# First block of x normed in two token halves, the gate's two bank readers put in a fixed order, and the last output weights spread over three rings

## The chip, the cores and the metric

The kernel runs on one core of one Trainium2 chip. The metric is the device time of one execution in microseconds. The names of the engines: PE is TensorE (matrix products; its weight loads are listed apart as PEld), DVE is VectorE, ACT is ScalarE, POOL is GpSimd, and SP is SyncE, which only issues transfers. Each engine works through its own queue in the order in which the program lists the instructions; engines wait for each other through semaphores.

## The reference

The program is one layer of a hybrid decoder trunk: 4096 tokens of width 1024, float32.

```
h = rmsnorm(x, norm_w);  u = h @ w_in
GLA   (4 heads): log_a = log_sigmoid(lr @ gate_up + bias) / 16
                 o = chunked gated linear attention(q, k, v, log_a);  o = rmsnorm(o) * silu(g)
RWKV7 (8 heads): token shift, low-rank decay w and rate a,
                 S_t = S_{t-1}(diag(w) - kk^T (a kk)) + v^T k;  y_t = S_t r_t
                 y = groupnorm(y) + bonus;  y = y * silu(g)
out = rmsnorm(x + concat(GLA, RWKV7) @ w_out, final_norm_w)
```

What matters here is that the input projection needs the normed x of a block, that the norm of a token needs a sum over all 1024 columns of that token alone, and that the gate of the linear attention is a log-sigmoid, which the kernel builds from min(z, 0) and from ln(1 + exp(-|z|)).

## The kernel before, in words

Tokens are processed in 8 blocks of 512 (`TB`). x is held transposed: a block is 8 tiles (`KT`) of 128 columns by 512 tokens. The product with float16 operands is kept accurate by splitting each operand into a high and a low float16 part: a projection of 128 output columns is three passes (high by high, high by low, low by high) over 8 tiles, and each step is two matmuls of 128x64 weights by 512 tokens that share the array (`both`, L894 in the profile; L833 is the helper that records every other instruction).

Weights come raw from memory in 29 pieces of 512 KB in the first block. Each is scaled by a power of two of its absolute maximum (an ACT pass over it, `wo<-x` in the profile since it uses an output buffer as scratch; a small PE transposition `bank<-identb,amW`; a few one-column DVE instructions that end in `scl`), split into high and low (ACT writes the high part `wr` or `wg`, DVE the low part), and stored to memory (`wdr`) for the seven later blocks. The raw tiles use the room of the second block's x (they appear as `x<-in_wt_dram`). RWKV weights go through the ring `wr` of two pairs, GLA weights through the ring `wg` of two pairs, output weights through the ring `wo` of two.

The first block's x is loaded in 8 tiles (named `mgg` and `mgr`, whose room it borrows), squared by ACT, summed over columns by PE, put through a reciprocal square root of seven DVE instructions (`newton`), spread over 128 partitions by PE, multiplied in by DVE, cast to the high part by ACT; the low part is a subtraction by DVE for even tiles and POOL for odd ones. Later blocks do the same with other loads, out of the way.

Per block there are then: the RWKV units (4 per block, `rwkv_ab`), whose chunked recurrence `rwkv_c` is a chain of small products with copies between them (`us`, `uv` by ACT, `sv` by DVE, all on bank `ch`); the GLA pairs (2 per block, `gla_proj` and `gla_pair`); and the output projection (`out_block`). The last block has its own output stage `out_last`, which multiplies the first six merged tiles while the last two units' chains are still running and adds the other two tiles at the end.

In `gla_pair` the gate is read twice from one bank of PSUM: DVE makes `gbc` = min(z + b, 0), and ACT makes `gep` = |z + b|, then exp and ln. The framework does not let two engines read one bank at the same time; the one whose instruction comes second in the program waits for the other.

The order of the program is not that of the code. Every instruction is first recorded as a step with what it depends on; a table (`ORDER`) holds a rank for each step, and the program is written out by taking, of the steps whose predecessors are out, the one of lowest rank. A second table (`STARTS`, counted by `COUNTS`) fixes how the streams (x, weights, RWKV, chain, GLA, output) interleave while steps are recorded. Both tables are data in the kernel. The first transfers out of the inputs, `lead`, are kept in their order; all other input loads come after them.

Of the kernel before, what the change touches and what calls it, by code (L numbers as in the profile page):

```python
# [27 lines left out]
TB = 512  # L28
C = 64
SPARE = 0.45  # L30
LAND = {"wdr": 1.5, "in": 1.7, "td": 1.3, "nd": 2.4, "kd": 2.2, "gd": 1.9}
ND = 20
NW = {"r": 4, "g": 4, "o": 2}
# [22 lines left out]
    "c-qx{2bd&f)oxXFoSZl3yeykoU<pf(lA}ll!2k#%2&hC81_VU~R1iTF$%;ylAIxC-$s*taE^%R5Hs_h?xplVQW509etE%pq;oj%&^VD`vb%igU_?~lydY+dFk3x9-r>CdK4?mNRVtC}kV<?Ud;XU=?=l_PErSO;;"  # L56
    "exHYHYr^A(@Z8bir~LNw@K_%na$iSyJQIFDKK%Se_&F~8{9E`LgrBE{M=m_>4F9e*?_U$1YcS_lhUc2ix#i)xw(zqa&ysU5h36)l>s}1cO*7~I6`q@sG7fV5IlOKd#!uf7;4?$l4RPEX;F`4<^E}SwF*e7A$L-;7"
    "AH@05;c;*H_g>*=_|bEr>2m@1O1qy8f0Open7)SRZxJ3Z;QPq%Sd6iriu2j<b3}N&5q_6;O$v{HW3F1m<6+!8Cp={Qvv{XG>kd3CgQJKxNqgF8Oal5%k8$Sjy6})S(vG$q7Jfbwe(sFl_YA*(Cp=E1=MKSpb?r#I"
    "zKu4?Sk~hAuJBwp`jNxma{d&Ylk0yI9<ynF<ovYo_ZM+a*3W$yUu|<eeyhPD=f;}$JuMp`{P!7La|Xt6GL20w=2^ba46l{;eG_9m9QVmJjkreo){gJXO3_-mJG^Hf%-1KdR<;U1r-YxY!q1Hu7a8X>%zkg8?^(>9"
    "KY*hpJa)zS$XaMd`}4FGM&MKa{#*t0r;;OxIbV-CZ9xCKK(l;|;|h$89OH3qhxycT56rrj&$)gyZnMLOj>0_Y+LV3ya!+)A60UzV{Cj(>_aBCbT)QuxCu4Pf_?)Z#=<i3v<FDc0<LRAB2ix&3A2eA%ziP%agL&1q"  # L60
    "XK9@m@Lkr+hj8w8+@Gmp>>KG_>%#koW6cf2cnd#}J`BUWx1%3F3y+=fzAVj`>m4_R*PTv0=+`ud9Tl`uX;2r9kF5PC!s7$sxwp{X8t{UoXYG{ou6mlUBg5l|3D3*Y9Lb(PDm-osuNVGSz}(CL?HU0ZeqVRAW_j&@"
    "BPfqyV}<iJqQdKBOm-iHJu1hI{n*z>R?v?_AaBUu6T|U&9W+qJZ7%lVgW)j-<K0Gk;*#*VJp64NSqnJ#Eyy(un7?MC`N|Xb4v&S9O@`yQBf{gl@SLoXKZKuOs)D|?IL?Xe(?R@RK1Z3q?S7A=hk3_udHR&Leh<I%"
    "9t-Gw!n?1J>C?W3*GpSgLC%wPJQ3@>0rJ~5J-un0w&gI$mNP(4WPXK*i(K<;%6M)=G)_LJVBY>f_vyS(BKoesO`^8TnmV1vKxt(_^r{{Fd<m_s5@gP=ho8#Zo9Ny3ShK+(?J1U{<a0-wuef)-8Z(ZqXshzPMPX+e"
    "tK<hsN7nq^8MY&jcedia3n05bjeWNXGU0RKr|1oH9Q=7Yo^ek2`wrkWDg$4cvSwNhy(yZ%WiDR{pRpgElXdXz@bkBzGe_ec>mB+_+A$KJwFx?djN9STf6(`-(4~_2PbEhy`XYMZ67Zd!{D?1?AS=t~AF7~Zg+X4|"
    "gLMcm_#XN(gvRy=$k4ZlJb-==$Gpq>oI^U~5wwQ)509UkapCooiJ4EK8T0Wj;j6crXS5jEDgYhZ2paP!XwW{;Zx;|<S{i<C!1s~Rr-l-3wa0mbBxk1`ho}60{vfZN9j*L`ahEl|m64xL4bR<%^}+OA^`R!{2{Z7$"
    "1%Hd}Vmh9&UHJWz3GK;%J_iYFBkgFQdzlw?l06|w2GGA}IiB54JT7n6OGfqt>CeBZfEJ85^dJkmGzNQ5X!JbLmk#_s6ZWX-ka5)ha3JWp%-uQQ1wQepCE&Alqzlb}t)^0*>7ro=n=!1%-agPg*R{8XnK58lx{2m)"
    "3)ozC7=-;-+mAKnT8Ddv1n^zxrn1&QjL*)<oYC_^KUxbV=qMTVX9TUG_drASnQgRY8@%%U!Y@Ap8Q>P8t)C)Wj{N<3qN}3g9&E-${+2eYU7-{9qyRFg?(I6-KP+=D!@VMBHX2!Z8S(T^^f^zmi_G=sOOc#D0rNW>"
    "*9&bIow~)0xsF*8ynGSHwgG%+HuS)4Np6z1oQm^b!F<01ex)*md_TOWH+{>d%>A?q<TRFn#m;s%uK8AYToL{)a>P(SYWL-(vQ6a#=#Im%Cr=5F=jr#8vDg1rp?nb#f6UM^jqEG!_*-Q8WAJR*yWcmmywy8+KXd<e"
    "4NeO0f8C5l#*F7<uv^MJel<MqFZJ%%HqdQky&e=EXJP*K#n=daJpnT11UzR;+$;LiAx4kkwgg6Il+TBVuk8~aO^$nRr!kPW9D()Ifb%~D?UQF5jWz!hdTthUt;ei87q3zpD0F%ojMc6<C*#qG{Z$KDYd7pCwY{E$"
# [362 lines left out]
def hymba_kernel(ctx, tc, xT, wt, wg, wo, wua, gup, pk, ck, out):  # L432
# [20 lines left out]
    def build(guide):  # L453

        TABLES = ("pkt", "scl", "invs", "hinv", "mu_s", "omu_s", "carry", "wosc", "woinv", "gnh", "lnh")
        FINE = {"Nb": 32, "f": 16}
        HEADS, XS = set(), set()
        now = [0.0]
        streams = []
        ready, used, busy = {}, {}, {}  # L460
# [126 lines left out]

        table = [0]
        steps, wkey, rkey, wlast, readers = [], {}, {}, {}, {}
        last, turn, lead = [None, 0], [0], []  # L590

        class Step:

# [1484 lines left out]
```

## Time and profile before

| | |
|---|---|
| time, median of 3 runs | 2169.9 us (2168.2 to 2171.18) |
| the profiled execution's own time | 2173.05 us |
| its span, first to last instruction | 2171.3 us |
| mean granted clock of TensorE | 0.991 |
| PE busy | 2107.4 us, 97% of the span |
| DVE, ACT, POOL busy | 1615.8, 1277.8, 892.8 us |
| moved by DMA | 322.27 MB, mean 148 GB/s |

How to read what follows: a row of the timeline has the start in us, how long it lasted, engine, source line, operation, what it writes and reads, shapes, count, and in brackets how long the engine had been idle before it and what ended that. `x12` is twelve like instructions run together. A row of the groups has busy us and the mean ns of one after the bar, then the idle time before them and who ended it. Matmuls are pipelined, so a busy PE is not yet PE at its peak.

### The profile page before, as it was taken

The page shows a single profiled execution, that of the slowest core. Times are in us where ns is not written, and L with a number is a line of the kernel's source. Part 1 is how long each engine was busy: PE and PEld are TensorE (multiplying, and loading weights), DVE is VectorE, ACT ScalarE, POOL GpSimd, SP SyncE. Part 2 cuts the span into 40 slices and gives each one's busy share as a digit, 9 for nine tenths or more (in the row PEclk, how much of TensorE's full clock was granted, in tenths as well). Part 3 has the DMA queues.
Part 4 walks back from the last instruction along what each step waited for, and adds up shares of the span by engine and source line. Part 5 has one row for each costly group of instructions (what it writes and reads, how often), then busy time and mean ns, then how long its engine had stood idle before and what let it go on. Part 6 is the DMA issues. An engine that isn't in the chain of part 4 may idle for free.

```text
span 2171.3 us, 68508 instructions
## 1 busy us (share of the span) xinstructions
PE 2107.4 (97%) x27608; PEld 1343.2 (62%) x27608; DVE 1615.8 (74%) x3487; ACT 1277.8 (59%) x3328; POOL 892.8 (41%) x2261
## 2 busy tenths in 40 slices
PE   6998999999999999999999999999999999999997
PEld 2655675565655657557675666656666565756664
DVE  8888979579675786757776687748868578685866
ACT  6777686465645556446664466545575555644552
POOL 4462434545414360545415264341544535254500
PEclk9999999999999999999999999999999999999999
DMA  6667655465344653445444464446533556344532
GB/s 196 203 176 234 207 177 176 137 194 158 94 128 128 189 150 96 133 129 187 144 110 129 135 195 131 126 120 184 163 103 103 162 166 178 88 131 129 151 108 88
DMA packets 271394, 322.27 MB, mean 148 GB/s; under 512 B 129588, under 2 KB 130788, under 8 KB 271076
## 3 DMA queue, kind: packets, MB, share of 16 engines
q1 hardware_dynamic: 271076, 317.89, 49.4%
q8 instruction: 216, 3.54, 0.7%
q14 instruction: 102, 0.84, 0.1%
HBM read 272.74 MB, written 45.05 MB: 146 GB/s over the span
## 4 chain that ended last, share of the span: by engine, by line
PE 80%; DVE 10%; ACT 4%; DMA 3%; issue 2%; POOL 1%; SPq 1%; DVEq 0%; ACTq 0%; POOLq 0%
PE bank L894 63%; PE bank L833 10%; PE ch L894 4%; PE y L894 1%; PE y L833 1%; DVE DD L833 1%; SPq L833 1%; DVE mgg L833 1%; ACT gep L833 1%; DVE bk L833 1%; DVE Nb L833 1%; DMA x<-in_wt_dram 1%; DVE gbc L833 1%; DVE x L833 1%; ACT L833 0%
## 5 line engine op out<-in xcount | busy, mean ns | idle before, releaser
L894 PE MATMUL bank<-x,wr 128*64 128x512 f16 x6528 | 817.0, 382 | 8.1 <-DVE DD L833 1.6
L833 POOL TENSOR_TENSOR tm<-Tc,f 128x60 f32<-128x60 f32 (+24 forms) x961 | 347.9, 362 | 534.6 <-DMA f<-nd 457.8
L894 PEld LDWEIGHTS <-wr 128*64 128x64 f16 x6528 | 360.2, 111 | 265.0 <-issue 26.8
L833 POOL TENSOR_TENSOR Tc<-Tc,tm 128x60 f32<-128x60 f32 (+24 forms) x961 | 359.3, 374 | 73.1
L894 PE MATMUL bank<-x,wg 128*64 128x512 f16 x3072 | 386.1, 381 | 2.4 <-ACT wg L833 1.7
L894 PE MATMUL bank<-x,wo 128*64 128x512 f16 x2976 | 356.1, 380 | 0.4 <-ACT x L833 0.4
L833 DVE SCALAR_TENSOR_TENSOR sv<-ch,PC,psd 64x64 f32<-64x64 f32 x434 | 122.6, 282 | 219.0 <-PE ch L894 185.8
L833 POOL TENSOR_TENSOR xacc<-xacc,xr 128x512 f32<-128x512 f32 x98 | 130.8, 1335 | 336.8 <-ACT xr L833 180.5
L894 PEld LDWEIGHTS <-wg 128*64 128x64 f16 x3072 | 167.6, 110 | 129.1 <-issue 7.9
L894 PEld LDWEIGHTS <-wo 128*64 128x64 f16 x2976 | 162.3, 110 | 120.1 <-issue 1.8
L894 PE MATMUL bank<-wg,x 128*64 128x256 f16 x3072 | 200.3, 273 | 0.3 <-ACT ta L833 0.3
L894 PEld LDWEIGHTS <-x 128*64 128x64 f16 x3168 | 170.4, 110 | 20.0 <-issue 3.4
L833 ACT COPY us<-ch 64x64 f32<-64x64 f32 x496 | 102.3, 206 | 122.7 <-PE ch L894 110.7
L833 ACT ACTIVATE psd<-sv,PC 128x128 f32<-128x128 f32 x248 | 98.8, 398 | 103.6 <-DVE sv L833 80.0
L833 ACT COPY uv<-ch 64x64 f32<-64x64 f32 x496 | 102.4, 206 | 86.4 <-PE ch L894 79.8
L833 ACT ACTIVATE sa<-bank,mu_s 128x512 f32<-128x512 f32 x104 | 71.5, 688 | 70.2 <-PE bank L894 64.3
L833 DVE COPY_PREDICATED Nb<-mc,bank 64x512 f32<-64x512 uint8 x128 | 92.9, 728 | 10.1 <-PE bank L833 8.0
L833 DVE COPY_PREDICATED DD<-mc,bank 64x512 f32<-64x512 uint8 x128 | 93.2, 729 | 2.7 <-PE bank L833 0.2
L833 POOL MEMSET Tc<- 32x8 f32 (+1 forms) x160 | 23.6, 147 | 173.1 <-DMA td<-Tc 167.7
L894 PEld LDWEIGHTS ch<-us,Nb 128*64 128x64 f32 x992 | 65.4, 137 | 42.5 <-ACT us L833 11.2
L894 PEld LDWEIGHTS ch<-uv,bk 128*64 128x64 f32 x992 | 66.8, 137 | 39.8 <-ACT uv L833 8.3
L894 PEld LDWEIGHTS ch<-sv,DD 128*64 128x64 f32 x992 | 66.0, 137 | 38.4 <-DVE sv L833 12.9
(354 smaller groups left out, 3584.0 us busy)
## 6 DMA issues: line engine op xcount, KB each, us to landing
wr<-wdr SPq DMA_DIRECT2D x248, 256.0 KB
xr<-in_xT_dram SPq DMA_DIRECT2D x176, 256.0 KB
wg<-wdr SPq DMA_DIRECT2D x176, 256.0 KB
wo<-wdr SPq DMA_DIRECT2D x128, 256.0 KB
f<-nd SPq DMA_DIRECT2D x128, 128.0 KB
x<-in_wt_dram SPq DMA_DIRECT2D x29, 512.0 KB
wdr<-wo SPq DMA_DIRECT2D x17, 512.0 KB
out_dram<-mgg SPq DMA_DIRECT2D x33, 256.0 KB
```

The lines of the kernel that those rows point to most:

```text
L833: put(t0, self.name, d, lag, cols, tiles, tab, outs, ins, lambda: f(*a, **kw))
L894: nc.tensor.matmul(x, lhsT=l, rhs=y, start=start, stop=stop)
```

## The change

Four things change.

- The first block of x is loaded, squared, summed, normed and split in two halves of 256 tokens (`TH`), by a new function `x_first`. The order of the first loads is: 8 halves (with the parameter table after the first), the first raw weight, the other 8 halves. Two Newton passes of 64 rows replace one of 128. The dependency keys of these tiles tell the two halves apart (`toks`, `TOK`). The first two RWKV projections (`NHALF = 2`) run in halves too, with the low weight before the low x.
- In `gla_pair` ACT's read of the bank is recorded ahead of DVE's. A new rule gives every step by DVE or ACT that reads a bank a dependency on the earlier readers of that bank by the other engine.
- In `out_last` the weights of the eight output columns take turns in the rings `wr`, `wg` and `wo` in place of `wo` alone.
- `ORDER`, `STARTS` and `COUNTS` are new, for the whole program. The counts of steps: RWKV stream 9609 to 9657, x stream 561 to 600, initial loads 35 to 44, weights 582 to 581.

```
-                if len(lead) <= KT:
+                if len(lead) < 2 * KT + 2:
...
+            for a in ins:
+                if a.space == PSUM and eng != "T":
+                    r = bankread.setdefault(a.tensor.name, [])
+                    for m in r:
+                        if m.eng != eng:
+                            s.follow(m, 0.1)
+                    r.append(s)
+            for a in outs:
+                if a.space == PSUM and eng == "T":
+                    bankread.pop(a.tensor.name, None)
...
+        for t in range(0, TB, TH):
+            for k in range(KT):
+                D.dma_start(xfirst[k][:, t:t + TH], xT[P * k:P * k + P, t:t + TH])
+                if k == t == 0:
+                    D.dma_start(pkt, pk)
+            if t == 0:
+                D.dma_start(raws[0], wt[W_WA])
...
+        def x_first():
...
+            for i, q in enumerate((lo, hi)):
+                ts = slice(TH * i, TH * i + TH)
                 ps = yield from need("X")
+                for k in range(KT):
+                    S.activation(sq[k][:, ts], xfirst[k][:, ts], AF.Square)
+                    for g in (2 * i, 2 * i + 1):
+                        T.matmul(ps[32 * g:32 * g + 32, 0:P], lhsT=gones, rhs=sq[k][:, P * g:P * g + P], start=k == 0, stop=k == KT - 1)
+                if i == 0:
+                    yield from norm_weight()
+                y = newton(ps[q, 0:P], 1.0 / DM, 1e-6, None, "g", q)
...
+                for k in range(KT):
+                    t = xfirst[k][:, ts]
+                    V.scalar_tensor_tensor(t, t, nwx[:, k:k + 1], rb[:, ts], ALU.mult, ALU.mult)
+                    S.copy(xs[k][:, 0, ts], t)
+                    (G if k % 2 else V).tensor_tensor(xs[k][:, 1, ts], t, xs[k][:, 0, ts], ALU.subtract)
...
+            early_ = st == "r" and made_r[0] < NHALF
+            made_r[0] += st == "r"
+            if early_:
+                for i in range(2):
+                    ts = slice(TH * i, TH * i + TH)
+                    for n, (a, c) in enumerate(((0, 0), (1, 0), (0, 1))):
+                        for k in range(kt):
...
+                            both(ps[:, ts], w[a][:, k, :], xs[k][:, c, ts], i + n + k == 0, i == 1 and n == 2 and k == kt - 1)
+                return ps
...
             bc, ep = tG("gbc"), tG("gep")
+            S.activation(ep, pz, AF.Abs, scale=gus[:, 5:6], bias=gb)
             V.tensor_scalar(bc, pz, gbz[:, j:j + 1], 0.0, ALU.add, ALU.min)
-            S.activation(ep, pz, AF.Abs, scale=gus[:, 5:6], bias=gb)
...
-                w = yield from get_w(NWT + n, "o")
+                w = yield from get_w(NWT + n, "o", ("r", "g", None)[n % 3])
```

More of the change, by code (lines that the diff above doesn't have):

```diff
@@ L28 @@
 TB = 512
+TH = TB // 2
 C = 64
@@ L32 @@
 ND = 20
+NHALF = 2
 NW = {"r": 4, "g": 4, "o": 2}
@@ L473, in dram, with toks @@
             return [(name, 0)]
+        def toks(ap):
+            t = ap.offset % TB // TH
+            return [t] if len(ap.shape) == 2 and ap.shape[1] <= TH and ap.dtype != BF16 else range(2)
         def parts(ap):
@@ L1902, in stream_w @@
             o = w_order()
-            for n in range(4):
+            for n in range(1, 4):
                 load_raw(n, o[n])
```

745 lines of the change are left out of this document (371 added, 374 removed).

## The prediction

> **What bounds the kernel now.** I read the page first, then the stretches of the start and of the clock drops, then TensorE's idle gaps, then the timeline around each gap.
>
> ```profile
> span 2171.3 us, 68508 instructions
> ...
> PE 2107.4 (97%) x27608; PEld 1343.2 (62%) x27608; DVE 1615.8 (74%) x3487; ACT 1277.8 (59%) x3328; POOL 892.8 (41%) x2261
> ```
>
> TensorE is idle for 2171.3 - 2107.4 = 63.9 us, and only those, with the stretches in which it runs slowly, are on offer. The busy time of stretches (PE, PEld, DVE, ACT, POOL, then granted clock, DMA share, GB/s):
>
> ```profile
> 807.50:810.90 3.40, 3.40 (x22) 1.70 (x20) 1.21 (x3) 3.06 (x7) 2.74 (x9) 0.50 0.00 0
> 1589.10:1592.50 3.40, 3.19 (x22) 1.79 (x24) 1.78 (x3) 3.30 (x8) 2.93 (x7) 0.50 0.00 0
> 2108.00:2111.40 3.40, 3.30 (x28) 1.88 (x28) 0.82 (x3) 1.61 (x8) 0.00 (x0) 0.51 0.09 31
> 0.00:20.00 20.00, 9.19 (x94) 4.17 (x95) 13.49 (x44) 11.37 (x19) 8.64 (x31) 1.00 0.92 262
> 20.00:37.40 17.40, 16.06 (x124) 6.27 (x121) 16.32 (x39) 10.17 (x19) 10.28 (x13) 1.00 0.59 185
> 37.40:47.34 9.94, 2.54 (x29) 0.82 (x24) 7.62 (x31) 9.75 (x18) 1.83 (x1) 0.78 0.25 90
> 47.34:53.10 5.76, 5.76 (x28) 2.56 (x30) 5.60 (x18) 5.68 (x9) 1.36 (x2) 0.50 0.60 161
> ```
>
> So there are two places to gain: the first 53 us (10.8 us idle before 20, 1.3 to 37.4, 7.4 to 47.34, then half clock), and short stalls later which each bring 3.4 us of half clock. In the first 37.4 us VectorE is busy 29.8 us: it bounds the start.
>
> **The change part by part.**
>
> *The gate's reads.* VectorE and ScalarE both read the gate's bank, 16 times. Whichever is listed second waits, and all that is queued behind it on its engine waits too; the old list did not hold that wait.
>
> ```profile
> L833 ACT ACTIVATE gep<-bank,pkt,gus 128x512 f32<-128x512 f32 x16 | 12.4, 775 | 18.4 <-DVE gbc L833 15.6 <-PE bank L894 2.7
> ...
> L833 DVE TENSOR_SCALAR gbc<-bank,gbz 128x512 f32<-128x512 f32 x16 | 11.9, 744 | 5.1 <-ACT gep L833 4.4 <-PE bank L894 0.6
> ```
> ```profile
> 805.00 0.75 DVE L833 TENSOR_SCALAR gbc<-bank,gbz 128x512 f32<-128x512 f32 x1
> ...
> 805.78 0.78 ACT L833 ACTIVATE gep<-bank,pkt,gus 128x512 f32<-128x512 f32 x1 [3.88 <-DVE gbc L833]
> ...
> 807.06 0.34 PE L894 MATMUL ch<-us,Nb 128*64 128x64 f32 x4 [2.48 <-ACT us L833]
> ```
> ```profile
> 1584.11 0.78 ACT L833 ACTIVATE gep<-bank,pkt,gus 128x512 f32<-128x512 f32 x1 [2.32 <-DVE gbc L833]
> ...
> 1589.31 0.48 PE L894 MATMUL ch<-us,Nb 128*64 128x64 f32 x4 [2.12 <-ACT Nb L833]
> ```
> ```profile
> PE bank L894 <- ACT gep L833: 1.1, 2, 0.7
> ```
>
> At 805.78 ScalarE had stood 3.88 us; the chain's copy `us` was behind it, and TensorE stood 2.48 us for that copy. At 1584 the same wait pushed the copies of `Nb` back, 2.12 us of TensorE. Each is followed by 3.4 us at 0.50, worth 1.7 us of lost work. Two more gaps are 1.1 us. Upper bound of the gain: 2.48 + 1.7 + 2.12 + 1.7 + 1.1 = 9.1 us. After the change ScalarE reads first, and VectorE is listed behind its end; behind VectorE's read are queued the chain's `sv` updates. The price of that order shows in the 4.4 us of the second row, and I bound the loss by them, +4. That the waits become visible to whoever made the list does not abolish 0.78 us of ScalarE, so not all comes back: I take **-5.5** (-9.1 to +4).
>
> [...]
>
> *The first block in halves.* Before:
>
> ```profile
> 8.03 0.63 ACT L833 ACTIVATE ta<-mgg 128x512 f32<-128x512 f32 x1 [1.05 <-DMA mgg<-in_xT_dram]
> ...
> 10.64 0.63 ACT L833 ACTIVATE uv<-mgr 128x512 f32<-128x512 f32 x1
> ...
> 12.04 0.29 DVE L833 TENSOR_SCALAR nva<-bank 128x128 f32<-128x128 f32 x1 [2.14 <-PE bank L833]
> 12.13 1.06 ACT L833 ACTIVATE wo<-x 128x1024 f32<-128x1024 f32 x1 [0.86 <-DMA x<-in_wt_dram]
> ...
> 19.17 3.90 PE L894 MATMUL bank<-x,wr 128*64 128x512 f16 x12 [1.40 <-ACT x L833]
> ...
> 28.98 1.28 DVE L833 SCALAR_TENSOR_TENSOR wr<-x,scl,wr 128x1024 f16<-128x1024 f32 x1
> ...
> 30.32 3.86 PE L894 MATMUL bank<-x,wr 128*64 128x512 f16 x34 [0.73 <-DVE wr L833]
> ```
>
> The fourth 256 KB tile, 1 MB in all, was there at 8.03. Eight halves are the same 1 MB, so their last square ends at 8.03 + 0.5 = 8.5. From the last square's end at 11.27 to Newton took 0.77 us; so the first Newton starts at 9.3, some 2.8 us ahead of 12.04. The first raw weight passes 1 MB of x in the list; between 4 and 12 us some 0.3 MB moved per us (rows under the rivals), so it is ready about 3 us ahead of 12.13. The first projection's matmuls thus start near 15 in place of 19.17.
>
> What is added, by the nearest rows of 256 columns:
>
> ```profile
> L833 ACT ACTIVATE guw<-f,gus 128x256 f16<-128x256 f32 x1 | 0.5, 494 | 0.0
> L833 DVE SCALAR_TENSOR_TENSOR guw<-f,gus,guw 128x256 f16<-128x256 f32 x1 | 0.5, 479 | 0.0
> ```
> ```profile
> L833 DVE SCALAR_TENSOR_TENSOR mgg<-mgg,nwx,bank 128x512 f32<-128x512 f32 x5 | 3.5, 739 | 0.0
> ...
> L833 ACT CAST x<-mgg 128x512 f16<-128x512 f32 x5 | 3.0, 614 | 0.2
> ```
>
> VectorE: 16 x 0.48 - 8 x 0.74 = 1.8 us for the products, a second Newton of seven instructions, the first of 0.29 (2 us), some 0.5 us for its four residues in halves: +4.3 us. ScalarE: 16 x 0.49 - 8 x 0.63 for the squares and 16 x 0.49 - 8 x 0.61 for the casts, +5.7 us. GpSimd's four residues become eight; it is idle 11 of the first 20 us. ScalarE has 8.6 us idle in the first 20 us and takes its share there. VectorE has 6.5 idle us there, 2.2 of them between 8 and 12 (1.78 busy of 4, rows under the rivals); leaving out the first 2 us, before any load has landed, some 4 stand against 4.3 added, so VectorE breaks even at 28.98, where the low part of a weight is made. So the gain has to come from TensorE: at 30.32 it still had 16 + 48 matmuls of the first two projections, 64 x 3.86 / 34 = 7 us, in front of the transposes that the third weight's scale waits for, and the part of them whose halves are ready before 30 is now done by then.
>
> The two projections in halves take 192 matmuls of 256 columns for 96 of 512:
>
> ```profile
> L894 PE MATMUL bank<-x,wg 128*64 128x512 f16 x3072 | 386.1, 381 | 2.4 <-ACT wg L833 1.7 <-DVE scl L833 0.4 <-ACT gep L833 0.4
> ...
> L894 PE MATMUL bank<-wg,x 128*64 128x256 f16 x3072 | 200.3, 273 | 0.3 <-ACT ta L833 0.3
> ```
>
> Busy time by count, two of 0.065 us stand for one of 0.126: 96 x 0.004, under 0.4 us.
>
> Then the third projection, where the start loses most:
>
> ```profile
> 42.55 0.75 DVE L833 TENSOR_SCALAR gbc<-bank,gbz 128x512 f32<-128x512 f32 x1 [1.85 <-ACT gep L833]
> ...
> 44.79 0.14 DVE L833 TENSOR_SCALAR scl<-pw 128x1 int32<-128x1 int32 x1
> ...
> 46.15 1.13 ACT L833 ACTIVATE wr<-x,scl 128x1024 f16<-128x1024 f32 x1
> ...
> 47.34 6.27 PE L894 MATMUL bank<-x,wr 128*64 128x512 f16 x30 [0.72 <-ACT wr L833]
> ```
>
> The scale at 44.79 stood behind the gate's read on VectorE, 1.85 us. That is the wait the list now knows. I take that, and as much again for the matmuls done early and the shorter half clock (at most (53.1 - 47.34) / 2 = 2.9): **-3.5**. Bounds: everything lost after 37.4, 7.4 + 2.9 = 10.3 less, and +4.3 if all of VectorE's added work is on the path. On SP eight more issues stand ahead of the second raw weight; its matmuls run after 30.32, so I add nothing for them, and +4.3 holds that too.
>
> *The last output weights.* Two buffers before:
>
> ```profile
> 2100.17 1.86 SPq L833 DMA_DIRECT2D wo<-wdr  x2
> ```
> ```profile
> 2104.75 0.41 PE L894 MATMUL bank<-x,wo 128*64 128x512 f16 x2
> ...
> 2109.00 1.49 PE L894 MATMUL bank<-x,wo 128*64 128x512 f16 x6
> ...
> 2149.95 5.82 PE L894 MATMUL bank<-x,x 128*64 128x512 f16 x48 [0.38 <-DVE mgr L833]
> ```
>
> From 2105.16 to 2109.00 no output matmul runs: two weights are used up and the third was issued at 2100.17. With six sets the third to sixth lie ready. But the last unit's chain ends at 2149.95 in a wait for VectorE, so filler moved forward mostly turns into a wait there. Gain between 0 and 3.84 plus 1.7 of half clock, 5.5; loss bounded by 1, a weight's load that now stands ahead of another transfer. I take **-1**, near the row of 2149.95.
>
> *The new list elsewhere.* It replaces every queue's order. The trace has no row for it. Its gaps outside the rows above (63.9 - 10.8 - 1.3 - 7.4 - 2.5 - 2.1 - 1.1, some 39 us, the end included) can grow or shrink; I bound that by a sixth of them either way, -6 to +6, and take 0, having no row that leans.
>
> Sum: -5.5 - 3.5 - 1 + 0 = -10. The profiled execution took 2173.05 us (span 2171.3 and 1.75 around it), 3.15 over the median of 2169.9: 2173.05 - 10 - 3.15 = **2159.9, forecast 2160**.
>
> **The rivals.**
>
> *Halves that come late.* The first half may not land at 8: it is eight transfers of 128 KB.
>
> ```profile
> 4.00:8.00 4.00, 2.21 (x26) 0.77 (x26) 3.86 (x5) 1.60 (x4) 4.00 (x9) 1.00 0.95 296
> 8.00:12.00 4.00, 3.24 (x40) 1.00 (x40) 1.78 (x12) 3.14 (x5) 0.78 (x5) 1.00 1.08 363
> ```
>
> For it: the DMA engines are full there, share 0.95 to 1.08. Against it: with several tiles in flight the rate is 296 to 363 GB/s, and the bytes are the same. If the rate halves, 1 MB lands 3.5 us later, the 2.8 us are gone and VectorE's 4.3 us stay: the start term is 0, the time 2163.5. [...]
>
> *No change.* The stalls return as planned waits and the start is held by VectorE: gate -1.5, start 0, tail 0, 2168.4. For it: VectorE's 29.8 of 37.4 us; ScalarE stays first at the gate and its queue is as long. Against it: 807.06 and 1589.31 are unplanned stalls of one cause.
>
> *Slower.* VectorE's added 4.3 us and half of ScalarE's 5.7 fall on the path to the third weight, since ScalarE is busy 9.75 of 9.94 us before 47.34: the split of 46.15 comes 7 us later, and 3 us more is lost as the half clock lasts that much longer. With 4 back at the gate: +6, 2176. It decides from where the third projection's dense run starts after 51. Against it: ScalarE's 8.6 idle us earlier.
>
> *Much faster.* All stalls of the gate (-9.1), most of the start (-9): -18, 2152.
>
> **How the numbers follow.** Forecast 0.45, late halves 0.18, no change 0.14, slower 0.14, much faster 0.09. Under 0.2%, about 4.3 us, this kernel's measurement cannot tell from no change. Faster by more: 0.45 + 0.18 + 0.09, less 0.03 of the edges, 0.69; within: 0.14 + 0.03 = 0.17; slower: 0.14. The range leaves out the end of the slow case and of the fast: 2149 to 2175.
>
> **What would show it.** Right: the first 256-column matmul before 16 us; the third projection's run before 44; ScalarE's idle before `gep<-bank` without VectorE as releaser, and no 2 us gap before `us`; no hole in the output matmuls. Wrong: VectorE's idle before `gbc<-bank` over 15 us with `sv` late behind it; the third projection after 51; new TensorE gaps over 1 us away from the gate.

## The result, and the profile after

The changed kernel took **2147.26 us** (median of 4 runs, 2145.91 to 2148.72) against 2169.05 (4 runs, 2167.94 to 2171.18) of the kernel before on the same chip: ratio 0.9898, with a 95% interval of 0.9881 to 0.9916. The gain is 21.8 us, twice the forecast 10, and the time is 1.7 us under the low end of the range. The direction was right.

The head of the page of the changed kernel, and its group rows for the gate (L852 now stands for L833, L913 for L894):

```profile
span 2146.8 us, 68755 instructions
...
PE 2095.0 (98%) x27704; PEld 1351.5 (63%) x27704; DVE 1619.2 (75%) x3506; ACT 1286.9 (60%) x3344; POOL 873.3 (41%) x2265
...
L852 ACT ACTIVATE gep<-bank,pkt,gus 128x512 f32<-128x512 f32 x16 | 12.4, 776 | 8.9 <-PE bank L913 8.7
...
L852 DVE TENSOR_SCALAR gbc<-bank,gbz 128x512 f32<-128x512 f32 x16 | 11.9, 745 | 4.4 <-ACT gep L852 4.1
```

TensorE is idle for 2146.8 - 2095.0 = 51.8 us where it was 63.9, and its busy time fell by 12.4 us although it does as much work. The clock is not the reason: the mean granted clock is 0.991 in the profiled execution of each kernel. What shortened the busy time the profile does not tell. ScalarE no longer waits for VectorE at the gate (15.6 us before), and VectorE's wait for ScalarE did not grow (4.4 before, 4.1 of the 4.4 now). What is left of ScalarE's idle time there is a wait for the matmuls themselves.

The start of the changed kernel, TensorE's timeline:

```profile
15.97 0.52 PE L913 MATMUL bank<-x,wr 128*64 128x256 f16 x6
...
44.43 5.37 PE L913 MATMUL bank<-x,wr 128*64 128x512 f16 x48 [0.70 <-ACT wr L852]
...
53.23 5.15 PE L913 MATMUL bank<-x,wg 128*64 128x512 f16 x32 [3.43 <-ACT wg L852]
...
61.94 0.48 PE L852 MATMUL bank<-DD,bk 64*128 64x128 f32 x2 [1.78 <-DVE bk L852]
...
63.62 3.43 PE L852 MATMUL bank<-DD,bk 64*128 64x128 f32 x30 [1.20 <-DVE bk L852]
```

The first projection starts at 15.97 in place of 19.17 and the third at 44.43 in place of 47.34. Behind them stand three waits, 6.4 us together. In the same place, the kernel before has one of 1.52, and its long wait stands ahead of the third projection:

```profile
46.30 0.32 PE L894 MATMUL bank<-identb,amW 128*64 128x128 bf16 x2 [4.14 <-ACT wo L833]
...
63.00 2.56 PE L894 MATMUL bank<-x,wg 128*64 128x512 f16 x22 [1.52 <-ACT wg L833]
```

The trace alone does not say what each of the four parts is worth; the runs below do.

The kernels named here: `gate_alone` is the kernel before with the gate's part only; names with `undone` are the changed kernel less one part. Where two kernels are compared step by step, the start times of like instructions of ScalarE and VectorE were paired and the median difference taken in each stretch; that is called the lead. It compares one execution of each, not medians.

### The profile page after: what moved, and what is told of

Same layout as the page of the kernel before. It is cut to its first block, busy times and chain, and to the rows that moved or that the text cites. A ratio compares the mean times of both kernels' runs of the same rounds, so it can differ in the third digit from the quotient of the medians.

```text
span 2146.8 us, 68755 instructions
## 1 busy us (share of the span) xinstructions
PE 2095.0 (98%) x27704; PEld 1351.5 (63%) x27704; DVE 1619.2 (75%) x3506; ACT 1286.9 (60%) x3344; POOL 873.3 (41%) x2265
## 4 chain that ended last, share of the span: by engine, by line
PE 85%; DVE 7%; DMA 3%; ACT 2%; issue 1%; SPq 1%; DVEq 0%; ACTq 0%
PE bank L913 68%; PE bank L852 10%; PE ch L913 4%; PE y L852 2%; PE y L913 1%; SPq L852 1%; DVE DD L852 1%; DVE nva L852 1%; DMA wg<-wdr 1%; DVE nta L852 0%; DVE Nb L852 0%; DVE mgg L852 0%; DVE bk L852 0%; DVE x L852 0%; DVE wo L852 0%
## 5 line engine op out<-in xcount | busy, mean ns | idle before, releaser
L913 PE MATMUL bank<-x,wr 128*64 128x512 f16 (+1 forms) x6732 | 831.3, 378 | 3.7 <-DVE DD L852 1.7
L852 POOL TENSOR_TENSOR tm<-Tc,f 128x60 f32<-128x60 f32 (+24 forms) x961 | 347.6, 362 | 622.3 <-DMA f<-nd 465.1
L913 PEld LDWEIGHTS <-wr 128*64 128x64 f16 x6732 | 370.8, 111 | 251.7 <-issue 15.8
L913 PE MATMUL bank<-x,wg 128*64 128x512 f16 x3180 | 397.7, 382 | 4.6 <-ACT wg L852 4.1
L852 POOL TENSOR_TENSOR Tc<-Tc,tm 128x60 f32<-128x60 f32 (+24 forms) x961 | 343.0, 357 | 72.9
L913 PE MATMUL bank<-x,wo 128*64 128x512 f16 x2760 | 328.3, 380 | 0.0
L852 DVE SCALAR_TENSOR_TENSOR sv<-ch,PC,psd 64x64 f32<-64x64 f32 x434 | 122.7, 283 | 222.2 <-PE ch L913 179.7
L913 PEld LDWEIGHTS <-wg 128*64 128x64 f16 x3180 | 176.1, 111 | 133.0 <-issue 6.2
L852 POOL TENSOR_TENSOR xacc<-xacc,xr 128x512 f32<-128x512 f32 x98 | 128.0, 1306 | 299.9 <-ACT xr L852 174.7
L913 PEld LDWEIGHTS <-wo 128*64 128x64 f16 x2760 | 150.1, 110 | 115.5 <-issue 1.9
L913 PE MATMUL bank<-wg,x 128*64 128x256 f16 x3072 | 198.1, 273 | 0.3 <-DMA wg<-wdr 0.3
L913 PEld LDWEIGHTS <-x 128*64 128x64 f16 x3168 | 169.3, 110 | 18.6 <-issue 4.7
L852 ACT COPY us<-ch 64x64 f32<-64x64 f32 x496 | 101.9, 205 | 106.3 <-PE ch L913 95.2
L852 ACT ACTIVATE psd<-sv,PC 128x128 f32<-128x128 f32 x248 | 98.9, 399 | 99.9 <-DVE sv L852 86.1
L852 ACT COPY uv<-ch 64x64 f32<-64x64 f32 x496 | 102.0, 206 | 86.5 <-PE ch L913 78.8
L852 ACT ACTIVATE sa<-bank,mu_s 128x512 f32<-128x512 f32 x104 | 71.4, 686 | 65.2 <-PE bank L913 63.4
L852 DVE COPY_PREDICATED Nb<-mc,bank 64x512 f32<-64x512 uint8 x128 | 93.1, 728 | 7.3 <-PE bank L852 5.2
L852 DVE COPY_PREDICATED DD<-mc,bank 64x512 f32<-64x512 uint8 x128 | 93.4, 730 | 5.4 <-PE bank L852 3.1
L913 PEld LDWEIGHTS ch<-sv,DD 128*64 128x64 f32 x992 | 66.3, 137 | 39.9 <-DVE sv L852 9.4
L913 PEld LDWEIGHTS ch<-uv,bk 128*64 128x64 f32 x992 | 66.7, 137 | 35.8 <-ACT uv L852 3.8
L913 PEld LDWEIGHTS ch<-us,Nb 128*64 128x64 f32 x992 | 66.4, 137 | 35.2 <-ACT us L852 4.0
L913 PE MATMUL ch<-sv,DD 128*64 128x64 f32 x992 | 72.1, 224 | 3.0 <-DVE sv L852 2.2
```

Of the source, the lines that this page charges most:

```text
L852: put(t0, self.name, d, lag, cols, tiles, tab, outs, ins, lambda: f(*a, **kw))
L913: nc.tensor.matmul(x, lhsT=l, rhs=y, start=start, stop=stop)
```

## The experiments

### The gate alone, and the gate put back

`gate_alone` is the kernel before with the two reads swapped and the rule added, on the old list. There VectorE's read stood first at 8 of the 16 gates; at these the two trade places:

```
+            S.activation(ep, pz, AF.Abs, scale=gus[:, 5:6], bias=gb)
             V.tensor_scalar(bc, pz, gbz[:, j:j + 1], 0.0, ALU.add, ALU.min)
-            S.activation(ep, pz, AF.Abs, scale=gus[:, 5:6], bias=gb)
```

> The kernel before, with one part of the change: ScalarE's read of the gate's bank is recorded ahead of VectorE's and the rule for such reads is in; the list is the old one, so at the 8 of 16 gates where the old list had VectorE first, VectorE's read now stands directly behind ScalarE's. Theory G (the gate's order is what paid): the two long stalls, 2.48 and 2.12 us, and their half clocks go, 5 to 9 us less, about 2161. Rival L (the gain is that of the newly planned list, the order of two reads alone only moves a wait from ScalarE to VectorE): between 2167 and 2173, and new waits of VectorE for ScalarE of more than 4.4 us in all.

Measured: 2158.19 (5 runs, 2155.07 to 2160.63), the kernel before, measured beside it, 2170.15; ratio 0.9945 [0.9933, 0.9958]: **12.0 us** faster, more than the bound of 9.1. Its groups, and TensorE's waits for the chain's copy (us in all, times, longest), here (L885) and in the kernel before (L894):

```profile
L824 ACT ACTIVATE gep<-bank,pkt,gus 128x512 f32<-128x512 f32 x16 | 12.4, 774 | 4.5 <-PE bank L885 4.3
...
L824 DVE TENSOR_SCALAR gbc<-bank,gbz 128x512 f32<-128x512 f32 x16 | 12.0, 748 | 7.2 <-ACT gep L824 7.1
```
```profile
PE ch L885 <- ACT us L824: 2.1, 5, 0.6
```
```profile
PE ch L894 <- ACT us L833: 4.5, 6, 2.5
```

ScalarE's idle time before the read went from 18.4 to 4.5 us; VectorE's rose from 5.1 to 7.2 only. The lead of `gate_alone` over before grows by 4.1 us at 806, 1.2 at 1068, 3.6 at 1584, 2 at 1837 and 1.6 at 2043, 12.5 in all. The last of these is a stretch of half clock (3.41 us at 0.50) that before has and `gate_alone` has not, behind a wait of 1.88 us that both have; it is therefore not shown to come from the order of the reads.

`gate_swapped` is the changed kernel with the two lines in the old order, each pair trading places in the list, so that VectorE reads first at all 16 gates:

> The changed kernel with VectorE's read of the gate's bank recorded ahead of ScalarE's at all 16 gates; the two trade their places in the list, the rule stays, so ScalarE's read waits for VectorE's. Theory O (ScalarE must go first: behind its read stand the copies of the chain that TensorE waits for, and VectorE comes late to the gate): 8 to 15 us slower than the changed kernel, 2155 to 2162, with ScalarE idle more than 12 us before its reads for VectorE, and gaps of TensorE ahead of the chain's copies. Rival P (it only matters that the list knows the wait, whichever order): 2146 to 2151.

Measured: 2158.22 (6 runs, 2156.33 to 2161.58), ratio 0.9943 [0.993, 0.9956], so 11 us lost against the changed kernel.

```profile
L852 ACT ACTIVATE gep<-bank,pkt,gus 128x512 f32<-128x512 f32 x16 | 12.4, 777 | 17.9 <-DVE gbc L852 17.8
...
L852 DVE TENSOR_SCALAR gbc<-bank,gbz 128x512 f32<-128x512 f32 x16 | 11.9, 747 | 7.8 <-PE bank L913 7.1 <-PE ch L913 0.3
```
```profile
PE ch L913 <- ACT us L852: 4.1, 5, 2.1
...
PE ch L913 <- ACT Nb L852: 2.3, 2, 1.9
```

ScalarE's 17.8 us and TensorE's waits for `us` and `Nb` are back. Added to one kernel and taken from the other, the order of the two reads is worth 11 to 12 us: the part stands by itself and needs no new list. That the two figures agree so well is in part chance, since the one run turns 8 gates round and the other 16.

### The halves

`start_undone` is the changed kernel with the first block whole again, the first 900 steps of the list (some 95 us) in the old order. `start_alone` is the other way round: halves and the first 900 steps new, the rest of the kernel before.

```
-            if b == 0:
-                yield from x_first()
-                return
...
-ORDER = (changed kernel's)
+ORDER = (old rank up to step 900, changed kernel's rank behind it)
```

> The changed kernel with the first block of x normed whole again, as before: the first 900 steps (some 95 us) come in the old order, all others in the new one; the gate's order, the rule and the rings stay. The two traces put the start's worth at some 2.5 us (lost time up to 200 us 70.4 before, 67.8 after). Theory L (nearly all of the 21.8 us comes from the list behind the start): 2149 to 2152. Rival S (the halves bring most, by letting all that follows begin earlier): 2158 or more.

> The first block in halves as in the changed kernel, with the first 900 steps in the new order; everything behind them in the old order, with the old reads of the gate and two output weights at a time. Theory L: 2 to 4 us under the kernel before, 2165 to 2167, and the stalls near 805 and 1584 us are there again. Rival S: 2158 or less.

Measured: `start_undone` 2144.18 (4 runs, 2143.28 to 2145.85), ratio 0.9881 [0.9867, 0.9894], some 3 us faster than the changed kernel and so faster than both. `start_alone` 2176.03 (8 runs, 2172.2 to 2178.92), ratio 1.0026 [1.0015, 1.0036], 5.9 us slower than before. **The halves lose 3 to 6 us.** `after_again`, the changed kernel measured once more, shows the scatter:

> The changed kernel once more, beside the three others on the same chip: 2147, as before (2145.9 to 2148.7).

It took 2147.95 (4 runs, 2146.56 to 2150.18), ratio 0.9909 [0.9894, 0.9923]. From 40 us on, the stretches (us, then busy PE, PEld, DVE, ACT, POOL, granted clock, DMA share, GB/s) of the changed kernel, then of `start_undone`:

```profile
40.00:50.00 10.00, 8.64 (x70) 3.76 (x62) 9.35 (x32) 9.89 (x16) 1.17 (x2) 0.87 0.16 56
50.00:60.00 10.00, 6.77 (x50) 3.15 (x50) 9.74 (x12) 9.87 (x22) 1.52 (x2) 0.83 0.62 182
```
```profile
40.00:50.00 10.00, 4.87 (x34) 2.04 (x34) 8.06 (x30) 9.90 (x16) 0.53 (x1) 0.54 0.22 72
50.00:60.00 10.00, 9.92 (x88) 4.90 (x84) 8.06 (x16) 8.06 (x18) 2.35 (x2) 0.95 0.61 191
```

With halves TensorE is ahead between 40 and 50 and stands in the next ten. VectorE (9.35, 9.74) and ScalarE (9.89, 9.87) are both full, where `start_undone` leaves each some 1.9 us in the second stretch. The lead of the halves over `start_undone` is 0.5 to 3 us between 30 and 70; it has turned into a delay of 2.1 between 70 and 80 and of 4.7 between 170 and 310. The later part of that delay comes with two stretches of half clock, 3.41 us at 0.50 each, at 131 and 162 us, which neither `start_undone` nor the profile of `after_again` has; in `after_again` the delay is already 4.6 between 70 and 80.

### What fills the two engines

Two runs add work to `start_undone`, of which nothing is used: after each of the 8 products of the first block either 320 columns on VectorE (planned as 4.3 us; the eight took 5.72 us in the trace, three of them over 1 us each) or a copy of 256 on ScalarE (3.3 us).

```
+                nc.vector.scalar_tensor_tensor(store[("gg", F32)][1][:, 0:320], q, 1.0, q, ALU.mult, ALU.mult)
...
+                nc.scalar.copy(store[("gg", F32)][1][:, 0:256], q)
```

> The changed kernel with the first block whole (2144.2), plus 8 instructions of VectorE that nobody needs, each a product of 320 columns behind one of the 8 products of the first block, about 0.53 us each, 4.3 us in all: the work that the halves put on VectorE. Theory E (VectorE is the bound of the start until about 70 us, so added work comes out at the end): 2 to 4.5 us more, 2146 to 2149. Rival F (it is hidden as far as the third projection, as I forecast, and the halves lose by the short runs of TensorE at half clock): less than 1 us more.

> The same kernel with the first block whole (2144.2), plus 8 copies of 256 columns by ScalarE, one behind each product of the first block, about 0.4 us each, 3.2 us in all, near what the halves put on ScalarE. Theory E2 (ScalarE is a bound of the start as well, it is busy 36 of the 40 us from 30 on): 1.5 to 3 us more. Rival F2 (ScalarE waits for loads and for VectorE there and takes it up): less than 1 us more.

Measured: `dve_extra` 2150.95 (4 runs, 2150.01 to 2151.23), 6.8 us over `start_undone`; `act_extra` 2149.03 (4 runs, 2146.22 to 2150.76), 4.8 over by the medians, but by the lead only 0.9 to 2.2: its profiled execution was the fastest of the four, so the size is not sure. The third projection in `dve_extra`, then in `start_undone`:

```profile
52.09 4.48 PE L884 MATMUL bank<-x,wr 128*64 128x512 f16 x20 [0.72 <-ACT wr L823]
```
```profile
46.55 5.64 PE L884 MATMUL bank<-x,wr 128*64 128x512 f16 x30 [0.72 <-ACT wr L823]
```

Nearly all of VectorE's 5.7 us arrives at the third projection, which starts 5.5 us later: work added to VectorE here does lie on the path.

Taking work out is the counterpart. `after_drop` and `start_undone_drop` leave out VectorE's low parts of the even tiles of the first block (GpSimd writes zeros in their place, so the first 512 tokens are less exact); `after_pool` makes all low parts on GpSimd.

```
-                    (G if k % 2 else V).tensor_tensor(xs[k][:, 1, ts], t, xs[k][:, 0, ts], ALU.subtract)
+                    G.tensor_tensor(xs[k][:, 1, ts], t, xs[k][:, 0, ts], ALU.subtract)   # after_pool
+                    G.memset(xs[k][:, 1, ts], 0.0)                                       # after_drop, even k
```

> The changed kernel without the eight low parts of the first block that VectorE makes (even tiles, two halves each): GpSimd fills those low parts with zero instead, which waits for nothing. The output of the first 512 tokens is less exact by it. VectorE has 8 x 0.42 = 3.3 us less to do between 19 and 29 us. Theory E (VectorE sets the pace of the start, so its added work is what the halves lose): 2.5 to 4.5 us less than the changed kernel (2147.6 over both its runs), 2143 to 2145. Rival D (something else sets the pace behind the third projection, the loads of the weights or ScalarE): within 1 us of the changed kernel.

> The changed kernel with the first block whole (2144.2), without the four low parts of the first block that VectorE makes, filled with zero by GpSimd (the first 512 tokens are less exact). VectorE loses 2.02 + 1.57 + 1.09 = 4.7 us between 22.4 and 27.0 us. Theory E: 3 to 5.5 us less, 2138.7 to 2141.2. Rival D: 2143 to 2145.

> The changed kernel with all sixteen low parts of the first block made by GpSimd, in place of eight by VectorE and eight by GpSimd; VectorE is freed of 8 x 0.42 = 3.3 us between 19 and 29 us, GpSimd, which is mostly idle there, takes some 6 us more. Theory E: 1.5 to 4 us less than the changed kernel, 2143 to 2146. Theory F: within 1 us of it; if GpSimd becomes late with the low parts, up to 3 us more.

Measured: `after_drop` 2149.32 (4 runs, 2146.1 to 2149.65), no gain; `start_undone_drop` 2142.82 (4 runs, 2139.4 to 2145.18), 1.4 us under `start_undone` for 4.7 us of VectorE, within its scatter; `after_pool` 2149.6 (4 runs, 2147.18 to 2150.82), no gain, and TensorE then waits 1.61 us at 30.03 for a low part by GpSimd, so that run decides nothing. VectorE's time added costs; time taken out gives little. VectorE's low parts alone are therefore not what the halves lose by.

### The clock, and the place of one split

In the changed kernel more of the start runs at half clock. TensorE's work in all such stretches before 66.5, then `start_undone`'s only one:

```profile
sum 20.50, PE 16.89; mean PE 3.38
```
```profile
40.80:51.00 10.20, 5.13 (x28) 2.29 (x28) 9.03 (x35) 10.09 (x17) 0.04 (x1) 0.50 0.32 100
```

That is 16.89 us against 5.13. `after_fill` and `start_undone_fill` put matmuls into an unused bank where TensorE waits before 66 us, to keep the clock up.

```
+FILL = ((17, 18), (43, 5), (44, 22), (165, 15), (166, 11), (201, 28), (226, 14), (227, 9))   # after_fill
+FILL = ((33, 9), (34, 6), (41, 11), (116, 10), (117, 6), (126, 34), (178, 12))               # start_undone_fill
```

> The changed kernel, with small products that nobody needs (128 columns of a unit matrix, 2 of 128x64 weights each) put ahead of the instructions that TensorE waited for in the first 66 us: 18, 5, 22, 15, 11, 28, 14 and 9 of them, so many that they should last a little less than the wait. They keep TensorE at work while it waits, so that the clock stays up; nothing else moves. In the changed kernel 16.9 us of work ran at half clock before 66.5 us, in the same kernel with the first block whole 5.1 us. Theory F (the halves lose because the early work comes in short runs, each of which is followed by half clock): 3 to 6 us less than the changed kernel, 2141 to 2144. Theory E (the start is bound by VectorE and ScalarE; what TensorE does at half clock is waiting time in any case): less than 1.5 us less, 2146 or more.

> The changed kernel with the first block whole, and the same fillers in its own waits before 62 us (9, 6, 11, 10, 6, 34 and 12 of them). It has one stretch of half clock there, 40.8 to 51.0 us, with 5.1 us of work. By F: 1 to 2.5 us less than without fillers, 2142 to 2143. By E: no change, 2143.5 to 2145.

Measured: `after_fill` 2148.71 (4 runs, 2148.18 to 2152.01), ratio 0.9914 [0.9899, 0.9929]: nothing gained, although the granted clock of its four executions was 0.993 to 0.995 against 0.991 to 0.992 in `after_again`. `start_undone_fill` 2143.03 (4 runs, 2142.03 to 2143.06), ratio 0.9883 [0.9867, 0.99], about 1 us under `start_undone`, and measured beside `after_again`, whose range lies wholly above: of the kernels that compute all of the reference it is the fastest. TensorE's stretches and rows in `after_fill`:

```profile
25.10:62.66 37.56, 29.16 (x466) 1.00 0.42 141
62.66:69.50 6.84, 6.26 (x44) 0.50 0.56 156
```
```profile
52.87 3.64 PE L913 MATMUL bank<-x,wg 128*64 128x512 f16 x32 [1.87 <-ACT wg L852]
...
61.59 0.48 PE L852 MATMUL bank<-DD,bk 64*128 64x128 f32 x2 [2.51 <-DVE bk L852]
```

The run at 52.87 took 3.64 us in place of 5.15, at full clock, and started only 0.36 us earlier; the product on `bk` still came at 61.59. TensorE got faster and stood longer, so in this pair the clock does not set the pace up to 62.66. Behind that the fillers did not hold it: `after_fill` ran 6.84 us at half clock there, the changed kernel 3.41.

In another execution of the changed kernel the clock probably does lie on the path. In the profile of `after_again` the third projection is longer (TensorE's rows, then ScalarE's first row behind it):

```profile
44.33 8.11 PE L913 MATMUL bank<-x,wr 128*64 128x512 f16 x48 [0.47 <-ACT wr L852]
55.54 5.33 PE L913 MATMUL bank<-x,wg 128*64 128x512 f16 x32 [3.10 <-ACT wg L852]
```
```profile
52.54 0.69 ACT L852 ACTIVATE sa<-bank,mu_s 128x512 f32<-128x512 f32 x1 [2.30 <-PE bank L913]
```

The projection took 8.11 us in place of 5.37 at a granted clock of 1.00. At 0.50, from 47.34 in the kernel before, 28 such matmuls took 5.76 us, 0.206 each, against 0.112; the 2.74 us more are thus, as an estimate, half clock for some 6 of the 8.11. ScalarE stood 2.30 us for it, and the next run started at 55.54 in place of 53.23; by the lead this execution stays 2.3 to 2.6 us behind the first one until 140 us. VectorE and ScalarE, full in the first profile, are busy 7.38 and 7.57 us between 50 and 60 in this one. The clock alone is thus not what the halves lose by, since holding it up gained nothing in all; that it was part of the loss in this execution rests on the estimate, and how large a part it is on average is not shown.

`wg_early` moves one rank: ScalarE's high part of the first GLA weight, for which TensorE stands 3.43 us at 53.23, goes ahead of the decay's instructions. `x1_late` moves the squares and sums of the second block, which run in this stretch, behind 66 us.

> The changed kernel with one instruction moved: ScalarE's high part of the first GLA weight, for which TensorE stands 3.43 us at 53.23, goes ahead of the decay's first activation (48.23 us), so that it runs as soon as the weight's scale is there (49.1). Theory O (an unlucky place in ScalarE's queue is what the halves lose): the wait at 53.23 shrinks to 0.6 us and 1.5 to 3 us are gained, 2144.5 to 2146. Rival B (ScalarE and VectorE together set the pace between 30 and 64 us; what goes earlier pushes the next): the waits for `bk` near 62 and 64 us grow by as much, within 1 us of the changed kernel.

> The changed kernel with the eight squares of the second block's x by ScalarE (0.61 us each) and the sums of them by GpSimd moved back in the list behind the place of the fifth RWKV weight, out of the first 66 us; they are not wanted before some 200 us. ScalarE is freed of five squares, 3.0 us, between 34 and 62 us, and VectorE's `bk` (1.70 us each at 60.14, 0.69 at 54.91) no longer runs beside GpSimd's sums. Theory B: the waits of 3.43, 1.78 and 1.20 us fall to 4 us or less in all and 1.5 to 3.5 us are gained, 2144 to 2146. Rival N (the start is given back later whatever it gains): within 1 us.

Measured: `wg_early` 2147.6 (4 runs, 2146.25 to 2150.06), the same as the changed kernel; `x1_late` 2157.7 (5 runs, 2155.67 to 2160.42), 10 us slower. TensorE's long waits, first of `wg_early`, then of `x1_late`:

```profile
58.42 0.32 PE L894 MATMUL bank<-identb,amW 128*64 128x128 bf16 x2 [3.27 <-ACT wo L833]
67.28 3.02 PE L833 MATMUL bank<-DD,bk 64*128 64x128 f32 x20 [4.10 <-DVE bk L833]
```
```profile
103.93 0.32 PE L894 MATMUL bank<-identb,amW 128*64 128x128 bf16 x2 [4.70 <-ACT wo L833]
```

The wait of 3.43 us went (0.5 is left, at 51.50), and two others of 3.27 and 4.10 came, behind ScalarE and then VectorE: a wait that changes its place. In `x1_late` the waits at 61.94 and 63.62 are gone and the kernel is 2.8 us ahead at 70 to 80; the work that was put off then meets the next weights, and it is 12.8 behind by 110 to 120.

### The tail: rings and order

`tail_undone` is the changed kernel with the old ring of two and the old order from step 21,700 on (about the last 200 us). `rings_old_tail` has the new rings with the old order there, `rings_undone` the new order with the ring of two.

```
-                w = yield from get_w(NWT + n, "o", ("r", "g", None)[n % 3])
+                w = yield from get_w(NWT + n, "o")
```

> The changed kernel, but the last output weights use the ring of two alone and everything from step 21,700 on (the last 170 us) stands in the old order. If the rings and the order of the tail are worth what I forecast, 1 us more than the changed kernel, 2148; by the traces (idle at the end 15.3 before, 12.85 after, and a half clock at 2108 that is gone) 2 to 5 us more, 2149 to 2152. If the tail carries a good part of the gain, 2155 or more.

> The changed kernel with the last output weights in three rings, but everything from step 21,700 on in the old order, which loads the third weight late as if there were two buffers. The run with the old tail and the ring of two took 5 us more than the changed kernel. Theory R (the rings pay only with an order that uses them): 2151 to 2154. Rival Q (six buffers alone let the loads run ahead): 2147 to 2149.

> The changed kernel in its new order throughout, with the ring of two for the last output weights. A load listed early now has to wait until the weight before it in its buffer is used up, and all transfers listed behind it wait too. Theory R: the new order of the tail needs the rings; slower than the changed kernel by 5 us or more, 2153 or above. Rival Q2 (the order of the tail pays by itself): 2147 to 2150.

Measured: `tail_undone` 2152.47 (4 runs, 2149.19 to 2155.07), ratio 0.9917 [0.9904, 0.9931]: the tail gives **5.2 us**. `rings_old_tail` 2154.53 (5 runs, 2152.07 to 2157.38): rings with the old order give nothing. `rings_undone` 2164.61 (12 runs, 2160.5 to 2170.01), ratio 0.9979 [0.997, 0.9987]: the new order without the rings loses 17 us. The two belong together. The same distance from the end in the changed kernel and in `tail_undone` (busy PE, granted clock, DMA share, GB/s):

```profile
2046.80:2096.80 50.00, 49.06 (x748) 1.00 0.43 117
2096.80:2121.80 25.00, 25.00 (x312) 1.00 0.26 88
```
```profile
2052.00:2102.00 50.00, 48.35 (x698) 0.97 0.35 91
2102.00:2127.00 25.00, 23.38 (x292) 1.00 0.31 97
```

In the 75 us ahead of the last 25 TensorE works 74.06 in place of 71.73 us, at full clock: 2.3 us of waits and 50 x 0.03 = 1.5 us of clock. The last 25 us are alike (12.15 and 12.42 us of work). The remaining 1.4 us fit a stretch of 6.8 us at half clock at 2020, worth 3.4, which the profiled `tail_undone` has and the profiled changed kernel has not; two other profiles with the new tail have 3.4 us of it near there (`after_fill`, `after_drop`), so that part varies. Why the order needs the rings is seen in `rings_undone`:

```profile
2108.82 4.58 PE L894 MATMUL bank<-x,wo 128*64 128x512 f16 x22 [5.80 <-DMA wo<-wdr]
```

### The list between start and tail

`middle_alone` has the gate's part, the new order from step 900 to 21,700, the old start and the old tail.

```
+ORDER = (old rank up to step 900, changed kernel's rank to 21,700, old rank behind it)
```

> The gate's order and the rule, and the new order of steps from the 900th to the 21,700th (some 95 to 1990 us); the start in whole blocks, the tail in the old order with two output weights at a time. The run with the gate alone took 2158.2, the one with all but the halves 2144.2, the one with all but the tail 5 us more than the changed kernel. Theory A (the parts add up; the new order itself is worth what is left over): 2144.2 + 5 = 2149, thus 9 us under the gate alone, by fewer idle gaps of TensorE between 100 and 1990 us and fewer stretches at half clock. Rival B (the order of the middle is worth nothing, my forecast's 0, and the parts help each other): 2156 to 2160.

Measured: 2149.47 (4 runs, 2147.42 to 2149.84), ratio 0.9901 [0.9887, 0.9914]: 8.7 us under `gate_alone`. TensorE in the middle, in `gate_alone` and then in `middle_alone`:

```profile
100.00:2000.00 1900.00, 1881.68 (x24958) 1.00 0.51 149
```
```profile
100.00:2000.00 1900.00, 1887.03 (x25096) 1.00 0.51 150
```

5.35 us of the middle's waits are gone (before had 1876.49 in that window, so the gate's part had already given 5.2 there). The gain is no single stall: no wait in either is over 1.5 us, and those of 0.6 to 1.5 us went from ten, 9.96 us together, to six, 5.83 us.

## Why the prediction had the direction and not the size

All four terms were off: the gate by 6.5 us, the tail by 4.2 and the list by 8.7 too little, the halves by 6.9 with the wrong sign. The step that failed by most is the one that put the new list at 0. That the total is not further out is luck: with the halves as forecast, the other three parts would have made it some 29 us.

The parts as measured: gate -12.0, halves +3.1 (+3.8 by `after_again`), tail -5.2, the list elsewhere -8.7. With +3.4 for the halves they add up to -22.5, against -21.8 for the whole change. Against the prediction's terms:

| term | forecast (bounds) | measured |
|---|---|---|
| gate's reads | -5.5 (-9.1 to +4) | -12.0; put back, +11 |
| halves | -3.5 (-10.3 to +4.3) | +3.4; alone +5.9 |
| last output weights | -1 (-5.5 to +1) | -5.2, with their order |
| the list elsewhere | 0 (-6 to +6) | -8.7 |

**The gate: right mechanism, wrong size.** ScalarE's wait vanished with VectorE no longer its releaser, the waits for `us` went from 2.5 us at the longest to 0.6, and the order cost VectorE 2.1 us more of idle time. The step that failed is the upper bound: I added two stalls with their half clock and "two more gaps" of 1.1 us in all. It left out the places at 1068 and 1837 (3.2 us by the lead, where it had 1.1 for two more gaps), and the two stalls that it did count came to 7.7, close to its 8.0. The lead's further 1.6 at 2043 is a half clock that is not shown to be the gate's. The discount to -5.5, for a wait that stays although it is planned, was wrong: nearly all came back.

**The halves: wrong sign.** The early steps came nearly as written: first matmul at 15.97 (15 forecast), third projection at 44.43 (before 44 asked for), 2.9 us earlier. What failed is the step from there to the end: "as much again for the matmuls done early and the shorter half clock". I priced VectorE's and ScalarE's added work at the first 30 us and took what came after as TensorE's gain. But between 40 and 60 us ScalarE and VectorE have the next splits to make and are full in the first profile, and the earlier start is followed by waits at 53.23, 61.94 and 63.62; in the second profile the third projection itself took 2.7 us longer, by the estimate above at half clock for some 6 us, where the forecast had a shorter half clock. My own sign for being wrong, new gaps over 1 us away from the gate, showed. The slower rival set its point at a third projection after 51; that did not come, and yet the halves lose: the loss lies behind that point. Of the rivals for this term "late halves" and "no change" (start term 0 in both) are nearest in size. The second's cause, a start held by VectorE, fits `dve_extra`; the first's does not hold. Its transfers of 128 KB were not slow: the first half's Newton was reached at 9.45, where 9.3 was forecast:

```profile
9.45 0.28 DVE L852 TENSOR_SCALAR nva<-bank 64x128 f32<-64x128 f32 x1 [0.58 <-PE bank L852]
```

**The tail: mis-sized.** The bound 5.5 held and the cause of the gain was right (TensorE has no idle time between 2096.80 and 2121.80, and the rings do that only with the order that uses them). The step that failed is the reason for taking 1 of it: matmuls moved forward did not turn into a wait at the last unit. After the change TensorE waits 0.60 there for VectorE, and the last wait of 2.31 us for `nyg` is as long as before.

**The list: wrong to call it 0.** I had bounded it by a sixth of 39 us of waits. 5.35 us of waits in the middle alone went, close to that bound. The clock does not give the rest: it was granted at 0.992 in the profiled `middle_alone` and at 0.994 in `gate_alone`. The rest of the -8.7 is not told apart.

Of the rivals, "much faster" (2152) came nearest to the time, but of its two terms only the gate's -9.1 was exceeded; its -9 at the start was a loss, and the rest came from tail and list. "No change" fell with the gate: the stalls did not return as planned waits.

What stays open is which part of the halves' added work makes the loss. Shown is that it isn't the clock alone (`after_fill`), though by the estimate it added 2.3 us in `after_again`, not VectorE's low parts alone (`after_drop`), and not the place of one split (`wg_early`). That both engines are full between 40 and 60 us is shown for one execution; that they together cause the loss is argued from it.

## What to carry to other kernels

When two engines read one bank, try first the one whose queue holds what TensorE waits for next (here worth 11 to 12 us over 16 places), and price every place where it happens, and the clock drop where one follows (here 3.41 us at 0.50 behind the stalls of 2.48 and 2.12 us), small ones too. Before moving the start of a phase forward, follow the engines that feed its next phase: here VectorE and ScalarE were busy 9.35 and 9.89 of the 10 us from 40 on in the first profile, and TensorE, 2.9 us earlier at the third projection, then stood 6.4 us. Here the buffers without the order that uses them were worth nothing, and the order without the buffers was a loss.

## What the runs showed of the hardware

The half clock does not follow from the length of a gap alone. Before the product on `bk` TensorE stood 1.88 us for VectorE, in the kernel before and in `gate_alone` alike (the timeline row of before, then that of `gate_alone`):

```profile
2042.84 3.58 PE L833 MATMUL bank<-DD,bk 64*128 64x128 f32 x32 [1.88 <-DVE bk L833]
```
```profile
2029.59 2.06 PE L824 MATMUL bank<-DD,bk 64*128 64x128 f32 x32 [1.88 <-DVE bk L824]
```

In the one the same matmuls took 3.58 us at a granted clock of 0.50, in the other 2.06 at full clock. In `gate_swapped` a gap of 2.14 us cost no clock at all:

```profile
1315.03 0.34 PE L913 MATMUL ch<-us,Nb 128*64 128x64 f32 x4 [2.14 <-ACT us L852]
```

In the traces of the kernel before and of the changed kernel all changes of the granted clock lie a whole number of times 3.413 us apart. In the kernel before, half clock begins at 807.47, 1589.13 and 2043.10 and lasts 3.41 us each time; the steps between these are 229 and 133 times 3.413. The stretch of that length ahead of the drop at 2043.10, with the whole gap in it, and the drop, then two such stretches around the gap of `gate_alone` and two around that of `gate_swapped` (TensorE's busy time, then the granted clock):

```profile
2039.69:2043.10 3.41, 0.77 (x16) 1.00 0.24 74
2043.10:2046.51 3.41, 3.41 (x34) 0.50 0.00 0
```
```profile
2024.80:2028.22 3.42, 2.16 (x50) 1.00 0.59 188
2028.22:2031.63 3.41, 2.04 (x34) 1.00 0.00 0
```
```profile
1310.33:1313.75 3.42, 2.24 (x22) 1.00 0.66 205
1313.75:1317.16 3.41, 2.13 (x24) 1.00 0.33 127
```

TensorE was busy 0.77 us of the stretch ahead of the drop, and 2.04 to 2.24 us of each of the four behind which none came. The busy time is not all: in the kernel before a stretch with 2.19 us was followed by half clock, one with 1.82 was not:

```profile
59.95:63.36 3.41, 1.82 (x18) 1.00 0.00 0
63.36:66.78 3.42, 3.42 (x38) 1.00 0.48 122
2104.54:2107.95 3.41, 2.19 (x35) 1.00 0.75 225
2107.95:2111.36 3.41, 3.31 (x28) 0.50 0.11 37
```

By these figures 3.41 us at 0.50 cost up to 1.7 us of work, and where they fall differs between executions of one kernel: the first profile of the changed kernel has half clock at 131.40 and 162.12, that of `after_again` has not. What else decides it no run shows.

VectorE's product `bk` of 64x512 took 1.70 us each (3.43 for two) at 60.14 in the changed kernel, while GpSimd added `xacc`:

```profile
60.14 3.43 DVE L852 SCALAR_TENSOR_TENSOR bk<-ta,E 64x512 f32<-64x512 f32 x2
```
```profile
58.40 2.94 POOL L852 TENSOR_TENSOR xacc<-xacc,xr 128x512 f32<-128x512 f32 x2 [9.26 <-ACT xr L852]
61.70 1.31 POOL L852 TENSOR_TENSOR xacc<-xacc,xr 128x512 f32<-128x512 f32 x1 [0.36 <-ACT xr L852]
```

The mean of the same operation over 62 of them between 100 and 2100 us of the kernel before is 710 ns, so 1.70 is not its usual time. The kernel before has both cases side by side, the first beside such a sum (64.65 to 66.16) and the second beside none:

```profile
65.00 1.70 DVE L833 SCALAR_TENSOR_TENSOR bk<-ta,E 64x512 f32<-64x512 f32 x1
...
67.59 0.69 DVE L833 SCALAR_TENSOR_TENSOR bk<-ta,E 64x512 f32<-64x512 f32 x1
```
```profile
64.65 1.51 POOL L833 TENSOR_TENSOR xacc<-xacc,xr 128x512 f32<-128x512 f32 x1 [10.55 <-ACT xr L833]
```

In that trace two of the 64 such products ran beside a sum `xacc`: the one at 65.00, and one of 1.14 us at 439.87, beside the sum from 439.19 to 440.46. The other 62 took 0.67 to 0.81 us. Why it takes longer there no run shows.
